# Two column blocks per bank in the output projections, new planner estimates, and queries rotated before their norm, in an fp32 two-layer encoder trunk

## The chip, the cores and the metric

The kernel is one program on one core of a Trainium2 chip. The metric is the device time of one execution in microseconds (us), taken as the median over runs.

## The reference, cut to what matters

Two layers over a sequence of 256 rows of 1024 features, all in float32. Each layer is: half a SwiGLU feed-forward (2816 wide), a mixer, cross-attention to a memory of 256 rows, half a feed-forward. The first mixer joins differential attention and stick-breaking attention; the second is latent attention (MLA):

```python
def mla_mixer(h, w_dq, q_lat_norm, w_uq, w_dkv, kv_lat_norm, w_ukv, qk_norm_q, qk_norm_k, w_o):
    c_q = rms_norm(h @ w_dq, q_lat_norm)
    q = to_heads(c_q @ w_uq, MLA_HEADS)
    dkv = h @ w_dkv
    c_kv = rms_norm(dkv[..., :MLA_KV_RANK], kv_lat_norm)
    kv = to_heads(c_kv @ w_ukv, MLA_HEADS)
    ...
    q = rms_norm(q, qk_norm_q)
    q = jnp.concatenate([q[..., :MLA_NOPE_DIM], rope(q[..., MLA_NOPE_DIM:])], axis=-1)
    o = chunk_causal_softmax_attention(q, k, v, MLA_QK_DIM ** -0.5)
    return from_heads(o) @ w_o

def diff_stickbreak_mixer(...):
    ...
    mixed = jnp.concatenate([from_heads(oa), from_heads(ob)], axis=-1)
    return mixed @ w_out

def memory_cross_attention(...):
    ...
    return from_heads(o) @ w_o
```

A rotation of a head's 32 rotary features and the division of the whole head by its own norm commute, since the norm is one number per row and head.

## The kernel before

All products are made from two fp32r halves of each operand: `mm3` (L285) issues three matmuls, high by high (L286), low by high (L287), high by low (L288). Weights arrive by DMA in float32; `issue` (L237) splits each into `wh` (a cast on ScalarE, L250) and `wl` (a subtraction on VectorE, the last 512 columns of a mixer's weight on GpSimd, L252). Three weights have room at once (`HL`), so a weight's split waits for the last use of the weight three before it.

The residual x is kept feature-major: 8 blocks of 128 features by 256 rows. The output projection of each mixer and of each cross-attention is `out_g` (L653). It goes over the 8 output blocks (`dt`) and over groups of source tiles, each with an event that says when the group is there (4 groups in a mixer, 2 in a cross-attention). Each `dt` accumulates in a PSUM bank of its own, taken from the 3 banks of kind "mm" (`BANKS`; the eight banks are 3 "mm", 2 "s" for scores, 2 "t" for transposes, 1 "o"). The first three blocks are open at once and take each group as it comes; the other five go one at a time. After the last group of a block, `finish_dt` (L506) adds the bank to x on VectorE (L510), makes the high half of the next phase's operand on ScalarE (L481) and the low half on VectorE (L482), and squares x for the next norm (L522, summed on GpSimd at L530). Then `drop` hands the bank back.

Only TensorE's order is written out by the kernel. Each piece of work is a generator that yields what it needs (events, a weight, a bank) and a latency; `run` (L437) keeps a clock of its own, to which every matmul adds an estimate (`spend`), and takes the ready piece of the highest priority. When an event counts as signalled is set by the tables EST_X0, EST_X1, EST_AB and EST_MLA, in us behind the instruction that signals it. The other engines' instructions are ordered by the scheduler of the framework, in the order in which it believes they become ready, and each engine runs its list in that order. GpSimd's powers (`rsqrt`, L465 and L467) make the inverse roots.

In the MLA mixer, `keys` (L1259) norms a half of the keys (sums of squares L1274 and L1275, power L467, products L1288 and L1290), `turn_k` (L1297) transposes them and copies them out of PSUM on ScalarE (L1305). `queries` (L1312) takes one product of 128 rows and 4 heads: scaled copy out of PSUM (L1319) and squares (L1322) on ScalarE, sums of squares (L1324), an addition (L1325) and a 4-wide power for the norm, and the rotation: a product with the cosines on VectorE (L1332), two with the sines on GpSimd (L1334), their sum on VectorE (L1337). Only the norm's inverse root is kept apart: it enters in the softmax as a factor. `attend` (L1401) transposes the queries of two heads at a time (L767), copies them out on VectorE (L1409), and makes the scores (L1422), the softmax (L745 to L760), the transposes of the weights, and the values (L1455). The weights of this mixer come in the order of MLA_ORDER. In the first mixer, `stick` (L1034) and `scores` (L1112) do the two kinds of attention, `turn_o` (L1182) turns the differential output, and `mem_k` (L809) makes the memory's keys, whose norm is the product L827 before their transposes.

## Time and profile before

| | |
|---|---|
| median of 3 runs | 1087.91 us (1087.11 to 1088.03) |
| the profiled execution | 1090.49 us |
| its span in the trace | 1088.8 us |
| mean granted TensorE clock | 0.995 |
| busy share | TensorE 98%, VectorE 71%, ScalarE 60%, GpSimd 18% |
| instructions | 23382 |

The span runs from the first to the last instruction of the profiled execution; the 1.7 us that its own time is longer lie around it. Stretches named in the prediction are us from the start of the span: 196 to 333 the first mixer, 333 to 384 the first cross-attention, 384 to 734 two feed-forwards, 734 to 865 the MLA mixer, 865 to 916 the second cross-attention.

### The profile page before, as it was taken

The page shows a single profiled execution, that of the slowest core. Times are in us where ns is not written, and L with a number is a line of the kernel's source. Part 1 is how long each engine was busy: PE and PEld are TensorE (multiplying, and loading weights), DVE is VectorE, ACT ScalarE, POOL GpSimd, SP SyncE. Part 2 cuts the span into 40 slices and gives each one's busy share as a digit, 9 for nine tenths or more (in the row PEclk, how much of TensorE's full clock was granted, in tenths as well). Part 3 has the DMA queues.
Part 4 walks back from the last instruction along what each step waited for, and adds up shares of the span by engine and source line. Part 5 has one row for each costly group of instructions (what it writes and reads, how often), then busy time and mean ns, then how long its engine had stood idle before and what let it go on. Part 6 is the DMA issues. An engine that isn't in the chain of part 4 may idle for free.

```text
span 1088.8 us, 23382 instructions
## 1 busy us (share of the span) xinstructions
PE 1065.9 (98%) x9040; PEld 1046.5 (96%) x9040; DVE 769.4 (71%) x1866; ACT 655.4 (60%) x1775; POOL 192.5 (18%) x210
## 2 busy tenths in 40 slices
PE   9999999999989999999999999999989999999998
PEld 8899999998889999999999999999878999999998
DVE  5978766567867877776677777654678768777753
ACT  6666555576756765555565655555867567555542
POOL 1100001356245200000100000014861422000000
PEclk9999999999999999999999999999989999999999
DMA  8765555635346365545556555555342444555561
GB/s 291 248 223 209 195 198 186 195 116 161 111 126 199 107 219 179 211 177 198 185 194 219 193 215 179 202 186 161 110 131 64 144 145 167 205 190 198 184 220 63
DMA packets 50800, 193.36 MB, mean 178 GB/s; under 512 B 5760, under 2 KB 7552, under 8 KB 35584
## 3 DMA queue, kind: packets, MB, share of 16 engines
q1 hardware_dynamic: 50688, 191.86, 51.3%
q8 instruction: 71, 1.16, 0.4%
q14 instruction: 41, 0.34, 0.1%
HBM read 190.79 MB, written 1.05 MB: 176 GB/s over the span
## 4 chain that ended last, share of the span: by engine, by line
PE 87%; DVE 5%; ACT 2%; POOL 2%; DMA 2%; issue 1%; SPq 0%; DVEq 0%; ACTq 0%; POOLq 0%
PE mm L286 28%; PE mm L288 27%; PE mm L287 27%; DVE wl L252 2%; DMA wr<-wflat 2%; ACT slotf L754 1%; PE t L767 1%; POOL sm L467 1%; PE s L1422 1%; PE t L475 1%; PE s L892 0%; PE o L1455 0%; DVE sm L745 0%; ACT wh L250 0%; POOL sl L467 0%
## 5 line engine op out<-in xcount | busy, mean ns | idle before, releaser
L250 ACT CAST wh<-wr 128x256 fp32r<-128x256 f32 (+1 forms) x1216 | 441.2, 434 | 294.9 <-PE mm L287 237.8
L252 DVE TENSOR_TENSOR wl<-wr,wh 128x256 fp32r<-128x256 f32 (+1 forms) x1171 | 479.5, 464 | 122.1 <-ACT wh L250 117.1
L286 PE MATMUL mm<-xh,wh 128*128 128x256 f32 x1584 | 439.9, 278 | 3.8 <-DVE slotf L705 2.6
L288 PE MATMUL mm<-xh,wl 128*128 128x256 f32 x1584 | 437.6, 276 | 0.1
L287 PE MATMUL mm<-xl,wh 128*128 128x256 f32 x1584 | 437.4, 276 | 0.0
L286 PEld LDWEIGHTS mm<-xh,wh 128*128 128x128 f32 x1584 | 298.3, 188 | 5.0 <-issue 2.8
L287 PEld LDWEIGHTS mm<-xl,wh 128*128 128x128 f32 x1584 | 298.4, 188 | 0.6
L288 PEld LDWEIGHTS mm<-xh,wl 128*128 128x128 f32 x1584 | 298.1, 188 | 0.7 <-DVE wl L273 0.4
L286 PE MATMUL mm<-slotr,wh 128*128 128x256 f32 x896 | 247.6, 276 | 0.3 <-ACT slotr L481 0.3
L287 PE MATMUL mm<-slotr,wh 128*128 128x256 f32 x896 | 246.6, 275 | 0.4 <-DVE slotr L482 0.4
L288 PE MATMUL mm<-slotr,wl 128*128 128x256 f32 x896 | 246.5, 275 | 0.0
L286 PEld LDWEIGHTS mm<-slotr,wh 128*128 128x128 f32 x896 | 168.2, 188 | 1.0 <-ACT slotr L481 0.6
L287 PEld LDWEIGHTS mm<-slotr,wh 128*128 128x128 f32 x896 | 168.2, 188 | 0.7 <-DVE slotr L482 0.6
L288 PEld LDWEIGHTS mm<-slotr,wl 128*128 128x128 f32 x896 | 168.2, 188 | 0.0
L530 POOL TENSOR_TENSOR acc<-acc,sq 128x256 f32<-128x256 f32 x49 | 38.7, 790 | 455.0 <-ACT sq L522 452.9
L252 POOL TENSOR_TENSOR wl<-wr,wh 128x512 fp32r<-128x512 f32 x45 | 67.4, 1497 | 110.3 <-ACT wh L250 92.2
L713 DVE TENSOR_TENSOR slotf<-mm,rb 128x512 f32<-128x512 f32 x44 | 30.4, 690 | 59.4 <-PE mm L288 59.4
L481 ACT ACTIVATE xh<-x,gains 128x256 fp32r<-128x256 f32 x64 | 32.1, 507 | 29.8 <-DVE x L510 25.8
L705 DVE TENSOR_TENSOR slotf<-mm,rb 128x512 f32<-128x512 f32 x44 | 30.3, 689 | 23.4 <-PE mm L288 23.2
L754 ACT ACTIVATE slotf<-s,sm,sl 128x256 f32<-128x256 f32 (+1 forms) x64 | 32.8, 522 | 23.3 <-DVE sm L748 17.8
L510 DVE SCALAR_TENSOR_TENSOR x<-mm,x 128x256 f32<-128x256 f32 x64 | 26.7, 418 | 23.5 <-PE mm L288 23.3
L482 DVE SCALAR_TENSOR_TENSOR xl<-x,gains,xh 128x256 fp32r<-128x256 f32 x64 | 37.5, 590 | 5.3 <-ACT xh L481 5.2
(196 smaller groups left out, 1152.7 us busy)
## 6 DMA issues: line engine op xcount, KB each, us to landing
wr<-wflat SPq DMA_DIRECT2D x118, 1024.0 KB, 4.9
wr<-wflat SPq DMA_DIRECT2D x180, 256.0 KB, 3.9
wr<-wflat SPq DMA_DIRECT2D x16, 768.0 KB, 4.2
slotf<-memT SPq DMA_DIRECT2D x8, 256.0 KB, 3.4
x<-xT SPq DMA_DIRECT2D x4, 256.0 KB, 4.9
wr<-wflat SPq DMA_DIRECT2D x2, 512.0 KB, 8.2
slotf<-xtok SPq DMA_DIRECT2D x4, 256.0 KB, 7.8
...
```

What stands on the lines that cost most here:

```text
L250: A.copy(hi[:, a:b], raw[:, a:b])
L252: e.tensor_tensor(out=lo[:, a:b], in0=raw[:, a:b], in1=hi[:, a:b].bitcast(F32), op=ALU.subtract)
L286: PE.matmul(out, a[0], b[0], start=first, stop=False, **kw)
L287: PE.matmul(out, a[0], b[1], start=False, stop=False, **kw)
L288: PE.matmul(out, a[1], b[0], start=False, stop=last, **kw)
L481: return (A.activation(hi, src, AF.Identity, scale=g), V.scalar_tensor_tensor(out=lo, in0=src, scalar=g, in1=hi.bitcast(F32), op0=ALU.mult ...
L482: V.scalar_tensor_tensor(out=lo, in0=src, scalar=g, in1=hi.bitcast(F32), op0=ALU.mult, op1=ALU.subtract))
L510: V.scalar_tensor_tensor(out=xd, in0=ps, scalar=factor, in1=xd, op0=ALU.mult, op1=ALU.add)
L530: G.tensor_tensor(out=st.acc, in0=st.acc, in1=sq, op=ALU.add)
L705: V.tensor_tensor(out=t.rearrange("p (a b) -> p a b", b=S), in0=pg.rearrange("p (a b) -> p a b", b=S), in1=rbb, op=ALU.mult)
L713: V.tensor_tensor(out=u.rearrange("p (a b) -> p a b", b=S), in0=pu.rearrange("p (a b) -> p a b", b=S), in1=rbb, op=ALU.mult)
L754: A.activation(p[:, i * w:(i + 1) * w], sps[:, i * w:(i + 1) * w], AF.Exp, bias=nb[:, i:i + 1], scale=r, accum_out=sums[:, i:i + 1])
```

## The change

`out_g` puts two neighbouring 256-column blocks into one 512-column bank. The start flag is set only by the first matmul of the even block, the bank is dropped after the odd block, and six blocks are open at once before the other two go one at a time. The estimates of the planner get new values, two latencies in `mem_k` and `turn_k` as well, the f32 slots of the MLA arena go from 29 to 30, and MLA_ORDER brings both first query weights ahead of the second key/value weight. In `queries` the rotation now comes first, in spare columns of z and sq, the sums of squares behind it, and one addition and one 8-wide power serve both row blocks of a query group (four 8-wide powers for eight 4-wide ones).

```diff
-SLOTS_MLA = (29, 11)
+SLOTS_MLA = (30, 11)
-EST_AB = {..., 'va': 1.47, ..., 'sp': 3.0, ..., 'srco': 1.25}
+EST_AB = {..., 'va': 2.8, ..., 'sp': 4.4, ..., 'srco': 2.2}
-MLA_ORDER = (('k', 0), ('kv', 0), ('kv', 1), ('q', 0), ('q', 1), ('k', 1), ('q', 2), ('q', 3), ('v', 0))
+MLA_ORDER = (('k', 0), ('kv', 0), ('q', 0), ('q', 1), ('kv', 1), ('k', 1), ('q', 2), ('v', 0), ('q', 3))
...
-        spend(3 * 0.109 * b[0].shape[-1] / 256)
+        spend(3 * 0.115 * b[0].shape[-1] / 256)
...
             w = ws[dt // per]
             j = dt % per
+            ps = pss[dt // 2]
             for i, k in enumerate(rows_):
-                mm3(pss[dt][:, 0:S], (w[0][:, k, j * P:(j + 1) * P], w[1][:, k, j * P:(j + 1) * P]),
-                    src[i], g == 0 and i == 0, g == len(groups) - 1 and i == len(rows_) - 1)
+                mm3(ps[:, dt % 2 * S:dt % 2 * S + S], (w[0][:, k, j * P:(j + 1) * P], w[1][:, k, j * P:(j + 1) * P]),
+                    src[i], g == i == dt % 2 == 0, g == len(groups) - 1 and i == len(rows_) - 1,
+                    skip_group_check=True)
...
-                ps = pss.pop(dt)
-                finish_dt(dt, gc, ps[:, 0:S])
-                drop(ps, 0.8)
-        nw = BANKS["mm"]
+                finish_dt(dt, gc, ps[:, dt % 2 * S:dt % 2 * S + S])
+                if dt % 2:
+                    drop(ps, 0.8)
+        nw = 2 * BANKS["mm"]
...
-                    yield dict(after=[ev], w=keyf(dt // per), mm=int(g == 0))
+                    yield dict(after=[ev], w=keyf(dt // per), mm=int(g == 0 and dt % 2 == 0))
...
-            yield dict(t=1, lat=7.0)
+            yield dict(t=1, lat=9.0)
...
-            v = sm()[:, 0:4]
-            V.tensor_reduce(out=v, in_=sq[:, 0:384]...)
-            V.tensor_scalar(out=v, in0=v, scalar1=96 * EPS, ...)
-            rsqrt(v, 4, rqs[n][:, t * 4:(t + 1) * 4])
...
-            m1 = tmp[:, 0:128].rearrange("p (a b) -> p a b", b=32)
-            m2 = tmp[:, 128:256].rearrange("p (a b) -> p a b", b=32)
+            m1 = z[:, 384:512].rearrange("p (a b) -> p a b", b=32)
+            m2 = sq[:, 384:512].rearrange("p (a b) -> p a b", b=32)
...
             V.tensor_tensor(out=qr, in0=m1, in1=m2, op=ALU.add)
+            V.tensor_reduce(out=qv[n][:, t * 4:(t + 1) * 4], in_=sq[:, 0:384]...)
+            if t:
+                v = qv[n][:, 0:8]
+                V.tensor_scalar(out=v, in0=v, scalar1=96 * EPS, ...)
+                rsqrt(v, 8, rqs[n])
```

EST_MLA changes in eleven places (k 6.43 to 9, q 7.82 to 8, qT 2.38 to 3, cs 3.11 to 2, sp 6.25 to 4.6, p1 3.36 to 4.4, p2 0.68 to 1.2, o 0.58 to 2.2, src 0.8 to 1.6, pk 2.4 to 1.6, kT 0.9 to 1.5), EST_X0 and EST_X1 in "o" (to 1.6) and "src" (8.83 to 2.0). Lines of the changed kernel behind `out_g` have numbers 4 or 5 higher: L1409 becomes L1414, L1290 becomes L1294; in `queries`, L1332 becomes L1331, L1334 becomes L1333, L1337 becomes L1336, and the sums of squares L1324 become L1337.

Three places of the order show what moved. The first is TensorE in the first mixer's output projection, where one output block ends (its last group) and the next one begins, before and then now; mm is the bank, slotr the source, wh and wl the weight's halves.

```order
L286 MATMUL mm_4082<-slotr_2682,wh_3889 128x256
L287 MATMUL mm_4082<-slotr_2682,wh_3889 128x256
L288 MATMUL mm_4082<-slotr_2682,wl_3890 128x256
L286 MATMUL mm_4089<-slotr_2682,wh_3889 128x256
L287 MATMUL mm_4089<-slotr_2682,wh_3889 128x256
L288 MATMUL mm_4089<-slotr_2682,wl_3890 128x256
```

```order
L286 MATMUL mm_4076<-slotr_2682,wh_3895 128x256
L287 MATMUL mm_4076<-slotr_2682,wh_3895 128x256
L288 MATMUL mm_4076<-slotr_2682,wl_3896 128x256
L286 MATMUL mm_4076<-slotr_2682,wh_3895 128x256 [waits DVE_49]
L287 MATMUL mm_4076<-slotr_2682,wh_3895 128x256
L288 MATMUL mm_4076<-slotr_2682,wl_3896 128x256
```

Before, the next block is in another bank (mm_4089 behind mm_4082). Now it is in the same one (mm_4076), and its first matmul waits for VectorE. The VectorE instruction that it waits for is the addition L510 of the block that has just ended.

The second is VectorE in the MLA mixer around the first copies of transposed queries, L1409 before and L1414 now; t is the transposes' bank.

```order
L1332 TENSOR_TENSOR slotf_9734<-slotf_9737,mqa 128x128 [waits Activation_49]
L252 TENSOR_TENSOR wl_10426<-wr_10424,wh_10425 128x512 [waits DMAHW3_49,PE_49,Activation_49]
L1324 TENSOR_REDUCE sm_10404<-slotf_9742 128x4 [waits Activation_49]
L1337 TENSOR_TENSOR slotf_9737<-slotf_9734 128x4x32 [waits DVE_49,Pool_49]
L1325 TENSOR_SCALAR sm_10404<-sm_10404 128x4 [waits DVE_49]
L252 TENSOR_TENSOR wl_10426<-wr_10424,wh_10425 128x512 [waits DMAHW4_49,Activation_49]
L1409 COPY slotf_9743<-t_10461 96x512 [waits PE_49]
L1409 COPY slotf_9740<-t_10467 96x512 [waits PE_49]
```

```order
L1331 TENSOR_TENSOR slotf_9741<-slotf_9741,mqa 128x128 [waits Activation_49]
L1336 TENSOR_TENSOR slotf_9741<-slotf_9741,slotf_9742 128x4x32 [waits DVE_49,Activation_49,Pool_49]
L1337 TENSOR_REDUCE sm_10268<-slotf_9742 128x4
L1331 TENSOR_TENSOR slotf_9743<-slotf_9743,mqa 128x128 [waits Activation_49]
L252 TENSOR_TENSOR wl_10301<-wr_10299,wh_10300 128x512 [waits DMAHW0_49,PE_49,Activation_49]
L1336 TENSOR_TENSOR slotf_9743<-slotf_9743,slotf_9744 128x4x32 [waits DVE_49,Activation_49,Pool_49]
L1337 TENSOR_REDUCE sm_10268<-slotf_9744 128x4
L252 TENSOR_TENSOR wl_10301<-wr_10299,wh_10300 128x512 [waits DMAHW1_49,Activation_49]
L1341 TENSOR_SCALAR sm_10268<-sm_10268 128x8 [waits DVE_49]
L1278 TENSOR_REDUCE sm_10340<-slotf_9721 128x8 [waits Activation_49]
L1414 COPY slotf_9722<-t_10355 96x512 [waits PE_49]
```

Before and now, the copy of the first query group's transposes (t_10461, now t_10355) stands behind the rotations of the second group; now the key's sum of squares L1278 stands ahead of it as well.

The third is GpSimd in the same stretch, from the weight half behind the first keys' products on.

```order
L252 TENSOR_TENSOR wl_10187<-wr_10185,wh_10186 128x512 [waits DMAHW3_49,PE_49,Activation_49]
L467 TENSOR_TENSOR sm_10223<-sm_10220,small 128x8 [waits DVE_49]
L1290 TENSOR_TENSOR slotf_9748<-slotf_9727,sm_10223 128x4x32 [waits Pool_49]
L1290 TENSOR_TENSOR slotf_9749<-slotf_9727,sm_10223 128x4x32
L467 TENSOR_TENSOR sm_10249<-sm_10246,small 128x8 [waits DVE_49]
L1290 TENSOR_TENSOR slotf_9729<-slotf_9727,sm_10249 128x4x32 [waits Pool_49]
L1290 TENSOR_TENSOR slotf_9730<-slotf_9727,sm_10249 128x4x32
L252 TENSOR_TENSOR wl_10269<-wr_10267,wh_10268 128x512 [waits DMAHW7_49,PE_49,Activation_49]
L1334 TENSOR_TENSOR slotf_9735<-slotf_9724,mqb 128x4x16 [waits Activation_49]
L1334 TENSOR_TENSOR slotf_9735<-slotf_9724,mqb 128x4x16
L467 TENSOR_TENSOR sl_10295<-sm_10298,small 128x4 [waits DVE_49]
```

```order
L1294 TENSOR_TENSOR slotf_9735<-slotf_9718,sm_10169 128x4x32
L252 TENSOR_TENSOR wl_10177<-wr_10175,wh_10176 128x512 [waits DMAHW3_49,PE_49,Activation_49]
L1333 TENSOR_TENSOR slotf_9737<-slotf_9736,mqb 128x4x16 [waits Activation_49]
L1333 TENSOR_TENSOR slotf_9737<-slotf_9736,mqb 128x4x16
L1333 TENSOR_TENSOR slotf_9740<-slotf_9739,mqb 128x4x16 [waits Activation_49]
L1333 TENSOR_TENSOR slotf_9740<-slotf_9739,mqb 128x4x16
L252 TENSOR_TENSOR wl_10242<-wr_10240,wh_10241 128x512 [waits DMAHW7_49,PE_49,Activation_49]
L467 TENSOR_TENSOR sl_10204<-sm_10203,small 128x8 [waits DVE_49]
L1333 TENSOR_TENSOR slotf_9742<-slotf_9741,mqb 128x4x16 [waits Activation_49]
```

Before, two more powers and four products for keys stand between the first weight half and the first rotation; now the rotations of the first query group follow it directly, and behind them another weight half, one 8-wide power and the second group.

## Rows read from the trace of the kernel before

**Rows 1.** The page, part 1: busy time and share of the span, instructions of TensorE.

```profile
PE 1065.9 (98%) x9040; PEld 1046.5 (96%) x9040; DVE 769.4 (71%) x1866; ACT 655.4 (60%) x1775; POOL 192.5 (18%) x210
```

**Rows 2.** Windows (stretch: length, PE, PEld, DVE, ACT, POOL busy, PEclk, DMA share, GB/s).

```profile
196.00:333.00 137.00, 130.31 (x1114) 125.41 (x1113) 97.02 (x180) 89.04 (x203) 63.66 (x59) 1.00 0.46 144
333.00:384.00 51.00, 50.43 (x409) 48.87 (x408) 39.56 (x97) 33.63 (x91) 17.43 (x17) 1.00 0.44 151
384.00:734.00 350.00, 350.00 (x3085) 349.89 (x3085) 249.06 (x631) 204.57 (x590) 12.67 (x15) 1.00 0.56 196
...
765.00:800.00 35.00, 30.10 (x186) 27.07 (x185) 22.11 (x48) 24.15 (x44) 29.97 (x32) 0.94 0.35 115
800.00:865.00 65.00, 62.98 (x488) 57.70 (x487) 53.84 (x136) 43.07 (x119) 20.13 (x23) 0.98 0.32 103
865.00:916.00 51.00, 50.43 (x410) 49.02 (x409) 38.97 (x97) 33.80 (x91) 17.60 (x18) 1.00 0.44 153
```

**Rows 3.** Windows around the two longest gaps of PE.

```profile
298.00:303.00 5.00, 2.77 (x25) 2.56 (x24) 4.10 (x6) 3.64 (x8) 4.20 (x4) 1.00 0.44 125
795.00:804.00 9.00, 8.01 (x33) 7.45 (x34) 7.43 (x17) 5.23 (x16) 4.67 (x4) 0.62 0.44 150
```

**Rows 4.** Waits of PE in 196:333 (us in total, times, longest).

```profile
PE t L767 <- DVE slotf L827: 2.2, 1, 2.2
PE s L323 <- ACT slotf L754: 1.9, 2, 1.0
PE o L1079 <- issue: 0.9, 1, 0.9
PE o L1079 <- ACT slotf L991: 0.9, 1, 0.9
```

**Rows 5.** Waits of PE in 734:916.

```profile
PE s L1422 <- DVE slotf L1409: 2.6, 1, 2.6
PE t L767 <- ACT slotf L1305: 1.4, 1, 1.4
...
PE o L911 <- DVE slotf L775: 0.6, 1, 0.6
```

**Rows 6.** Timeline of all engines, 317.2:319.9, the diff/stick mixer's output projection.

```profile
317.91 0.28 PE L288 MATMUL mm<-slotr,wl 128*128 128x256 f32 x1
...
318.02 0.28 PE L286 MATMUL mm<-slotr,wh 128*128 128x256 f32 x1
...
318.22 0.42 DVE L510 SCALAR_TENSOR_TENSOR x<-mm,x 128x256 f32<-128x256 f32 x1 [2.35 <-PE mm L288]
...
318.68 0.51 ACT L481 ACTIVATE xh<-x,gains 128x256 fp32r<-128x256 f32 x1 [3.68 <-DVE x L510]
```

**Rows 7.** Groups by line over the whole span (busy, mean ns; idle before).

```profile
L482 DVE SCALAR_TENSOR_TENSOR xl<-x,gains,xh 128x256 fp32r<-128x256 f32 x64 | 37.5, 590 | 5.3 <-ACT xh L481 5.2
```

**Rows 8.** Groups by line and shape, window 755:830 (busy, mean ns; idle before).

```profile
L252 DVE TENSOR_TENSOR wl<-wr,wh 128x512 fp32r<-128x512 f32 x23 | 18.9, 835 | 6.3 <-ACT wh L250 6.3
...
L252 POOL TENSOR_TENSOR wl<-wr,wh 128x512 fp32r<-128x512 f32 x9 | 12.5, 1391 | 4.0 <-ACT wh L250 4.0
...
L1334 POOL TENSOR_TENSOR slotf<-slotf,mqb 128x64 f32<-128x64 f32 x16 | 7.3, 476 | 12.8 <-ACT slotf L1319 12.8
L467 POOL TENSOR_TENSOR sm<-sm,small 128x8 f32<-128x8 f32 x4 | 6.9, 1730 | 1.9 <-DVE sm L584 0.9 <-DVE sm L1275 0.8
...
L1409 DVE COPY slotf<-t 96x512 f32<-96x512 f32 x8 | 5.3, 675 | 0.2 <-PE t L767 0.2
...
L1324 DVE TENSOR_REDUCE sm<-slotf 128x4 f32<-128x384 f32 x8 | 4.3, 541 | 0.0
...
L1274 DVE TENSOR_REDUCE sm<-slotf 128x8 f32<-128x512 f32 x4 | 2.7, 673 | 0.0
...
L1337 DVE TENSOR_TENSOR slotf<-slotf 128x128 f32<-128x128 f32 x8 | 2.2, 279 | 4.1 <-POOL slotf L1334 4.1
```

**Rows 9.** Timeline of POOL, 772.2:773.5.

```profile
772.28 1.18 POOL L1290 TENSOR_TENSOR slotf<-slotf,sm 128x128 f32<-128x128 f32 x2
```

**Rows 10.** Timeline of PE, 759.7:760.0, first product with the latent key/value weight.

```profile
759.73 0.39 PE L286 MATMUL mm<-wh,slotr 128*128 128x512 f32 x1
```

More of the change, by code (lines that the diff above doesn't have):

```diff
@@ L677, in out_g @@
                 for dt in win:
-                    yield dict(after=[ev], w=keyf(dt // per), mm=int(g == 0))
+                    yield dict(after=[ev], w=keyf(dt // per), mm=int(g == 0 and dt % 2 == 0))
                     if dt // per not in ws:
                         ws[dt // per] = weight(keyf(dt // per), per * P)
-                    if g == 0:
-                        pss[dt] = take("mm")
+                    if g == 0 and dt % 2 == 0:
+                        pss[dt // 2] = take("mm")
                     part(dt, g)
@@ L1306, in turn_k @@
                 kT[hf].append(d)
-                drop(pt, 0.9)
+                drop(pt, 1.5)
                 signal(ev["kT", hf, g], EST_MLA["kT"])
@@ L1315, in queries @@
             if t == 0:
-                qf[n], rqs[n] = [], sl()
+                qf[n], qv[n], rqs[n] = [], sm(), sl()
             z = al()
@@ L1322, in queries @@
             A.activation(sq[:, 0:384], z[:, 0:384], AF.Square)
-            v = sm()[:, 0:4]
-            V.tensor_reduce(out=v, in_=sq[:, 0:384].rearrange("p (a b) -> p a b", b=96), axis=AX.X, op=ALU.add)
-            V.tensor_scalar(out=v, in0=v, scalar1=96 * EPS, scalar2=None, op0=ALU.add)
-            rsqrt(v, 4, rqs[n][:, t * 4:(t + 1) * 4])
             qr = z[:, 0:384].rearrange("p (a b) -> p a b", b=96)[:, :, 64:96]
-            tmp = al()
-            m1 = tmp[:, 0:128].rearrange("p (a b) -> p a b", b=32)
-            m2 = tmp[:, 128:256].rearrange("p (a b) -> p a b", b=32)
+            m1 = z[:, 384:512].rearrange("p (a b) -> p a b", b=32)
+            m2 = sq[:, 384:512].rearrange("p (a b) -> p a b", b=32)
             ta, tb = tabs["mq"]
@@ L1337, in queries @@
             V.tensor_tensor(out=qr, in0=m1, in1=m2, op=ALU.add)
-            rel(sq, tmp)
+            V.tensor_reduce(out=qv[n][:, t * 4:(t + 1) * 4], in_=sq[:, 0:384].rearrange("p (a b) -> p a b", b=96),
+                            axis=AX.X, op=ALU.add)
+            if t:
+                v = qv[n][:, 0:8]
+                V.tensor_scalar(out=v, in0=v, scalar1=96 * EPS, scalar2=None, op0=ALU.add)
+                rsqrt(v, 8, rqs[n])
+            rel(sq)
             signal(ev["q", n, t], EST_MLA["q"])
```

10 lines of the change are left out of this document (5 added, 5 removed).

## The prediction

> **What bounds the kernel now.** I read the page first, then windows by stage, then TensorE's waits in the stages that are not full. TensorE is busy 98% of the span [rows 1], so only its idle time can be won, and the windows say where that is [rows 2]: the two feed-forwards between 384 and 734 have none (350.00 of 350), the first mixer has 6.7 us (137 less 130.31), each cross-attention 0.6 (51 less 50.43), the MLA mixer 4.9 and 2.0. To the MLA mixer a second loss belongs: TensorE ran at 0.62 of its clock from 795 to 804, between its levels of 2.4 and 1.2 GHz, which is 9 x 0.38 = 3.4 us [rows 3]. In all 6.7 + 1.2 + 6.9 + 3.4 = 18.2 us, 1.7% of the time, is the most that a better order can give.
>
> The waits name what is late. First mixer [rows 4]: 2.2 for the normed memory keys, 1.9 for two scores' banks, 1.8 for the stick-breaking values; 0.8 is in smaller waits. MLA mixer [rows 5]: 2.6 for a score behind the copy of its queries (L1409), 1.4 for a transposes' bank (L1305). In the cross-attention the wait is 0.6 at the values (L911).
>
> **Part 1, two blocks per bank.** The reader should look at the seam between an even block and its odd partner. Before, the last matmul of a block started at 317.91 and the first of the next block, in another bank, at 318.02 [rows 6]. Meanwhile L510 started at 318.22 and took 0.42, and the engine behind it started 0.04 after its end, at 318.68. Now the odd block's last group (or, for the two late blocks, its first) waits for that L510. TensorE can go on no earlier than 318.68 in place of 318.02: 0.66 per pair at least. The order shows such a wait at every pair: 4 pairs x 4 projections = 16, and TensorE has no other work between the two halves in any. The floor is 16 x 0.66 = 10.6 us.
>
> It costs more where VectorE isn't free. Lay out the first mixer's projection from the last matmul of block 0 at zero: L510 ends at 0.73, TensorE resumes at 0.77 and does block 1 (6 matmuls, 0.7) and block 2 (0.7), ended at 2.2. VectorE has by then L482 of block 0 (0.59 [rows 7], not before L481's 0.51: ended 1.9), L510 of block 1 (2.3), a weight piece (0.84 [rows 8]: 3.1), and only then L510 of block 2, ended 3.5. TensorE waits 1.3 instead of 0.66. By the same layout the third pair waits 1.0, and the fourth 1.5, as three weight pieces stand ahead of its L510: 0.7 + 1.3 + 1.0 + 1.5 = **4.5 us**. The MLA projection has the same order, one weight piece less at the end: **4.2**. The cross-attentions split their weights in smaller pieces: **3.2** each. Together 15.1, between 10.6 and, with one more weight piece of 0.84 ahead of half of the 16, 22.
>
> The Trainium skill (PSUM — Partial Sum Buffer, "PSUM bank collisions raise a hardware error") says that two engines may not touch one bank and quadrant at once, disjoint columns included, and tells to guard by bank, not by address. The instructions of the changed kernel are guarded so; a guard by address would take the 15.1 out of the sum. No run here shows a collision.
>
> What the six open blocks bring is small: the blocks' first groups no longer wait for a bank, so more matmuls are ready while the mixer's last source is made. In the cross-attentions the cover for the first source becomes thinner in layer 0 (6 matmuls) and better in layer 1: I take 1.5 of waits there for the two, where the two stretches had 1.2 idle [rows 2]. Cross-attentions: 0.3 + 6.4 = **+6.7 us**.
>
> **Part 2, the first mixer's order.** The longer latencies (9 for memory keys, 2.8 for "va", 4.4 for scores) put other matmuls ahead of the transposes and values that waited: 2.2 + 1.8 + 0.8 go, and one of the two waits for scores' banks (0.9) [rows 4]. New: a stick-breaking product has 12 matmuls less ahead of it and waits about 1.0 (0.3 to 2.5) for VectorE's halves, and a score's bank is behind a run of weight casts on ScalarE, 1.2 (0.5 to 2). One wait for scores stays, 1.0. The fourth weight chunk is released 24 matmuls (2.7 us) before its first use instead of 78; its third piece would come over 2 us late, but the seams just before hold TensorE back by as much, so I cost it at nothing. Idle after: 1.0 + 1.2 + 1.0 + 4.5 = 7.7 for 6.7: **+1.0**, between -4 and +3.
>
> **Part 3, queries and the MLA order.** Eight 4-wide powers become four 8-wide ones; as one of these takes 1.73 [rows 8], GpSimd saves little by it. What counts is its queue. Count from GpSimd's products for the first keys, ended 773.46 [rows 9], which the change leaves where they are. Then come, in the order shown, a weight half 1.39, four rotations 4 x 0.48, a weight half 1.39, a power 1.73, four rotations 1.90 [rows 8]: 782.2. VectorE adds the last rotation (0.28), reduces (0.54), splits a weight piece (0.84), adds the constant (0.16, an estimate: about half of L1337), reduces a key's squares (0.67) and then copies the first query group's transposes (0.68): 785.4.
>
> When does TensorE want that bank? The first product of the key/value weight starts at 759.73 [rows 10]. From there to the second transposes of queries the new order has 42 matmuls of 512 columns, 48 of 384 and 22 small ones; at 0.115 per 256 columns that is 9.7 + 8.3 + 2.5 = 20.5, so 780.2. It waits **5.2 us**, from 780.2 to 785.4: the planner's "q" and "qT" (8 and 3) don't know GpSimd's queue. Behind it the same again: the next copy stands behind a key's products that wait for GpSimd's next two powers (782.2 + 1.39 + 2 x 1.73 = 787.1, two products of about 0.54 and the copy: 788.8), wanted at 785.4 + 2.3 = 787.7: **1.1**. The third score then waits for a bank whose maximum stands behind two copies and three weight pieces on VectorE (1.35 + 2.5): **2.7**, between 1.3 and 3.5. After the 5.2 the clock falls to its lower level, as it did in the rows after the waits of 1.4 and 2.6; part of the 3.4 is hidden in the two waits that follow, I take **1.0**. What is late next: the values' sources and the last two sources of the projection have under 1 us of cover; I take **3.0** for the second half where the row has 2.0. With the banks 5.2 + 1.1 + 2.7 + 1.0 + 3.0 + 4.2 = 17.2 for 6.9 + 3.4 = 10.3: **+6.9**, between -3 and +13.
>
> Moved instructions on other queues: SP loads the query weights ahead of the second key/value weight, and the loads aren't late in any row that I rest on; the one extra f32 slot, the smaller change in `spend` and the two latencies in "src" act by the order only. The feed-forwards are not touched: nothing.
>
> **Sum.** +1.0 + 6.7 + 6.9 = +14.6 on the profiled execution's 1090.49: 1105.1. That execution is 2.6 us above the median of the runs, so 1087.91 + 14.6 = **1102.5 us**. Under 0.2% (2.2 us) a measurement can't tell from no change.
>
> **Rivals.**
> *The re-estimated order works* (slower still, by less). If GpSimd and VectorE take the queries before the weight pieces, so that the copy ends by 780.2, the waits of 5.2, 1.1, 2.7 and the clock's 1.0 are gone: 1102.5 - 10.0 = 1092.5. For it: the new latencies are longer where the rows show waits [rows 4, 5]. Against it: the queues in the order shown, each price from a row. Chance 0.17.
>
> *Faster.* One mechanism: the idle of the two mixers is all hidden and the seam costs its floor only. The place is the mixers, the price up to 18.2 won against 10.6 paid: 1087.9 - 18.2 + 10.6 = 1080.3. It decides at the point where more than the seams' cost is won; at 13 of the 18 it gives 1085.5. Against it: the waits counted above; the seam cannot be hidden, as TensorE takes its instructions in order. Chance 0.10.
>
> *The clock falls in the projections too.* There TensorE is busy 8.3 of some 12.8 us in the mixers. If it falls once in each, 2 x 3.4 more: 1109.3. For it: it fell after the gaps of 1.4 and 2.6 [rows 3, 5]. Against it: a stretch with a gap of 2.2 and 2.77 busy of 5.00 stayed at 1.00 [rows 3], and no seam is over 1.5. Chance 0.13.
>
> *The seam isn't there*, since VectorE's read is tracked by columns and the wait means an older instruction: 1102.5 - 15.1 = 1087.4, no change. Against it: the wait stands at each pair and at no other place of the block. Chance 0.04.
>
> **The numbers.** The forecast has 0.56, its own range 1096 to 1109. With the unknown prices (-5 and -10 in the mixers' own terms, +7 in seams and +6 in MLA, not all at once) and the second and fourth case, 1091 to 1113 holds 8 in 10. Faster by over 0.2%: 0.10; within 0.2%: 0.05, from the fourth case and the edge of the second; slower: 0.85.
>
> **What would show it.** Right: in the waits of the changed kernel PE mm L286 <- DVE x L510 with some 16 times and 10 to 20 us; PE t L767 <- DVE L1414 with one wait of about 5; the normed memory keys (L831) gone from the list. Windows: the cross-attentions' idle at 3 to 4 in place of 0.6. Wrong: an L510 wait of under 8 us in all, or no wait over 2 us before a transposition of queries; then the MLA term is off, and the sum with it.

## The result, and the profile after

| | before | after |
|---|---|---|
| median, us | 1087.51 (1086.38 to 1088.03, 4 runs) | 1117.39 (1116.01 to 1117.95, 4 runs) |
| the profiled execution | 1090.49 | 1116.01 |
| its span | 1088.8 | 1114.3 |
| mean granted clock | 0.995 | 0.992 |

The changed kernel takes 1.0266 times as long, with an interval of 1.0249 to 1.0283, which is 27 to 31 us more; the two medians are 29.9 us apart. The forecast was 14.6. The two traces differ by 25.5 us only: the profiled execution of before was 3.0 above its median, that of after 1.4 below its own. Where these 4.4 us lie can be read from the last L510 of the first feed-forward, in before and in after:

```profile
195.14 0.42 DVE L510 SCALAR_TENSOR_TENSOR x<-mm,x 128x256 f32<-128x256 f32 x1
```

```profile
190.70 0.42 DVE L510 SCALAR_TENSOR_TENSOR x<-mm,x 128x256 f32<-128x256 f32 x1 [0.16 <-PE mm L288]
```

Up to here TensorE's order is the same in both kernels, matmul by matmul, and yet the execution of before is 4.4 us behind. It had waited for VectorE near the program's start, and its clock fell behind that wait; in after the same wait is 0.3 and the clock is at 1.00 in the same window. The second fence is that window, with the columns of [rows 2]; the wait is the longest of before, though [rows 3] has two others as the longest:

```profile
30.02 0.35 PE L286 MATMUL mm<-xh,wh 128*128 128x256 f32 x1 [2.64 <-DVE slotf L705]
```

```profile
28.00:36.00 8.00, 5.98 (x38) 6.01 (x39) 7.65 (x22) 5.19 (x15) 1.19 (x5) 0.79 0.69 224
```

This is the spread of single executions and not the change: of the kernels below that leave all of this part as it is, the one with new estimates for the MLA attention alone passes the same L510 at 195.12, the one with the first mixer's new estimates at 190.84. From this point to the end, after takes 25.5 + 4.4 = 29.9 us longer than before, the distance of the medians. It is these 29.9 that have to be explained.

The page of after, part 1, answers to [rows 1]:

```profile
PE 1074.0 (96%) x9040; PEld 1051.1 (94%) x9040; DVE 776.5 (70%) x1862; ACT 656.6 (59%) x1775; POOL 191.6 (17%) x206
```

The windows of after answer to [rows 2, 3] (stretch: length, PE, PEld, DVE, ACT, POOL busy, PEclk, DMA share, GB/s). The stages are the first mixer, cross-attention, feed-forwards, the MLA mixer in two parts, cross-attention:

```profile
196.00:340.00 144.00, 135.34 (x1148) 129.97 (x1147) 101.41 (x186) 92.61 (x210) 64.75 (x62) 1.00 0.45 141
340.00:395.00 55.00, 51.22 (x398) 48.59 (x398) 39.64 (x99) 34.09 (x94) 12.79 (x12) 1.00 0.38 134
395.00:745.00 350.00, 350.00 (x3089) 349.85 (x3088) 248.34 (x628) 202.84 (x585) 16.82 (x19) 1.00 0.57 197
...
776.00:811.00 35.00, 26.38 (x141) 22.98 (x140) 25.93 (x56) 18.31 (x43) 19.31 (x22) 0.82 0.32 106
811.00:885.00 74.00, 63.97 (x482) 57.31 (x481) 52.01 (x117) 43.89 (x113) 21.38 (x22) 0.98 0.24 77
885.00:945.00 60.00, 56.83 (x445) 54.82 (x445) 43.07 (x102) 37.19 (x99) 19.36 (x19) 0.98 0.44 153
```

TensorE's idle time is length less busy. The feed-forwards have none, as before. The first mixer has 8.7 (before 6.7), the cross-attentions 3.8 and 3.2 (0.6 each), the MLA mixer 8.6 and 10.0 (4.9 and 2.0). The clock of 0.82 says that the MLA mixer lost more than idle time.

The waits of PE over the whole span of after (waiter <- what it waited for: us in total, times, longest), in place of [rows 4, 5]:

```profile
PE mm L286 <- DVE x L510: 15.7, 16, 2.3
PE s L323 <- ACT slotf L758: 3.5, 2, 2.8
PE t L771 <- ACT slotf L1309: 2.8, 1, 2.8
PE t L771 <- DVE slotf L1414: 2.8, 1, 2.8
...
PE t L475 <- POOL acc L530: 1.6, 2, 0.8
```

The first row is the seam of the prediction, with its 16 times: 15.7 us that no row of before has. The next three have one wait of 2.8 each in the MLA mixer. The last is new as well: at the end of each cross-attention the transposing matmul L475 of the next norm waits for GpSimd's sum of squares, which comes after the last seam.

The same view for the first mixer, 196 to 340, and for the first cross-attention, 340 to 395:

```profile
PE mm L286 <- DVE x L510: 5.5, 4, 2.3
PE s L1067 <- ACT slotr L486: 1.0, 1, 1.0
...
```

```profile
PE mm L286 <- DVE x L510: 2.4, 4, 0.8
PE t L475 <- POOL acc L530: 0.8, 1, 0.8
PE mm L287 <- DVE slotr L487: 0.6, 1, 0.6
```

The rest of the first mixer is 8.7 - 5.5 = 3.2, as forecast. The MLA mixer's seams are 5.5 too, the second cross-attention's 2.4.

Now the first mixer's four seams, one by one. The timeline of PE in after, 315.6 to 322.9 (start, us, engine, line, tiles; in brackets the idle before it and its releaser) shows three:

```profile
316.72 0.38 PE L286 MATMUL mm<-slotr,wh 128*128 128x256 f32 x1 [0.52 <-DVE x L510]
...
319.40 0.39 PE L286 MATMUL mm<-slotr,wh 128*128 128x256 f32 x1 [1.01 <-DVE x L510]
...
322.72 0.39 PE L286 MATMUL mm<-slotr,wh 128*128 128x256 f32 x1 [1.64 <-DVE x L510]
```

Such a wait is counted from the modelled end of the matmul before, not from the time at which the next one could start; from start to start each seam is 0.16 longer. The four are 0.68, 1.17, 1.80 and 2.50, together 6.15 where 4.5 was laid out. What VectorE did before the third, and GpSimd beside it (timelines of after):

```profile
319.26 0.48 DVE L482 SCALAR_TENSOR_TENSOR xl<-x,gains,xh 128x256 fp32r<-128x256 f32 x1
...
320.41 0.42 DVE L510 SCALAR_TENSOR_TENSOR x<-mm,x 128x256 f32<-128x256 f32 x1
320.75 1.58 DVE L482 SCALAR_TENSOR_TENSOR xl<-x,gains,xh 128x256 fp32r<-128x256 f32 x1
322.25 0.41 DVE L510 SCALAR_TENSOR_TENSOR x<-mm,x 128x256 f32<-128x256 f32 x1
```

```profile
320.78 1.27 POOL L252 TENSOR_TENSOR wl<-wr,wh 128x512 fp32r<-128x512 f32 x1 [15.36 <-ACT wh L250]
```

The low half L482 that starts at 320.75 takes 1.58 us; at 319.26 it takes 0.48. It ends 0.28 behind GpSimd's weight half (320.78 + 1.27 = 322.05), and the L510 for which TensorE waits starts then, at 322.25. Before the fourth seam it is two weight pieces on VectorE: 2.92 us from 325.46 where the usual is 1.36, beside GpSimd's next weight half (325.35 to 326.70) and the first of its sums L530 (326.66 to 327.83). L510, which reads one operand from PSUM, takes 0.41 to 0.43 throughout. This is what the Trainium skill (SBUF — State Buffer, "Who interferes with whom") states: a VectorE instruction with two inputs in SBUF contends with a GpSimd instruction that reads SBUF, one with at most one such input, outside the two-port modes, does not. The trace agrees on both halves of the rule. The same section of the Trainium skill calls this contention an exclusive lock. The trace agrees there too, as L482 ends only when GpSimd's instruction has ended.

The MLA mixer's three waits, in the timeline of PE:

```profile
785.29 1.94 PE L771 MATMUL t<-cst,slotf 128*96 128x128 f32 x8 [2.83 <-ACT slotf L1309]
...
791.90 1.94 PE L771 MATMUL t<-cst,slotf 128*96 128x128 f32 x8 [2.79 <-DVE slotf L1414]
...
805.68 0.47 PE L323 MATMUL s<-mk,mq 128*128 128x128 f32 x1 [2.81 <-ACT slotf L758]
```

The first, 2.83, was in no term of the sum. TensorE wants a transposes' bank and ScalarE has not copied the keys before it (L1309). The timeline of ScalarE and SP's load (SPq: from issue to landing):

```profile
782.17 0.62 ACT L250 CAST wh<-wr 128x512 fp32r<-128x512 f32 x1 [2.38 <-DMA wr<-wflat]
...
784.03 0.62 ACT L250 CAST wh<-wr 128x512 fp32r<-128x512 f32 x1 [0.31 <-DMA wr<-wflat]
784.55 1.25 ACT L1309 ACTIVATE slotf<-t,small 96x512 f32<-96x512 f32 x2
```

```profile
779.50 6.79 SPq L248 DMA_DIRECT2D wr<-wflat  x7
```

The keys' copy stands behind casts of weights, and these wait for a load that SP could issue only at 779.50, just after VectorE had read the buffer's old contents for the last time (until 779.41). The copy starts at 784.55, and TensorE 0.74 later. ScalarE's two waits for the load, 2.38 and 0.31, are together nearly as long as TensorE's 2.83. VectorE was held up there as at the seams: its last two pieces took 2.59 instead of 1.36 beside a weight half of GpSimd's.

```profile
776.82 2.59 DVE L252 TENSOR_TENSOR wl<-wr,wh 128x512 fp32r<-128x512 f32 x2
```

```profile
777.12 1.74 POOL L252 TENSOR_TENSOR wl<-wr,wh 128x512 fp32r<-128x512 f32 x1
```

The second wait is the predicted one, for the copy of transposed queries (L1414): 2.8 and not 5.2 + 1.1. Both of its ends came later than laid out, counted from the end of GpSimd's products for the first keys (777.15 here). TensorE wanted the bank 12.0 behind that point and not 6.7, mostly by the first wait and the fall of the clock behind it. The copy was done 14.7 behind it and not 11.9, as GpSimd didn't run through: its power waited 2.18 for VectorE's L1341.

```profile
783.94 2.21 POOL L467 TENSOR_TENSOR sl<-sm,small 128x8 f32<-128x8 f32 x1 [2.18 <-DVE sm L1341]
```

```profile
791.17 0.67 DVE L1414 COPY slotf<-t 96x512 f32<-96x512 f32 x1
```

The third is the score's bank: 2.81 for 2.7.

The clock, in windows at the four places of after, behind the program's start, where the granted clock went to its lower level (columns as above):

```profile
784.50:788.00 3.50, 2.71 (x11) 2.46 (x12) 1.41 (x4) 3.50 (x7) 3.50 (x6) 0.54 0.64 219
791.30:794.80 3.50, 2.90 (x11) 2.64 (x12) 1.47 (x4) 0.68 (x1) 3.42 (x4) 0.54 0.67 225
805.00:811.90 6.90, 6.22 (x25) 5.78 (x26) 4.23 (x15) 3.89 (x17) 0.00 (x0) 0.52 0.36 130
883.50:887.00 3.50, 3.50 (x20) 3.50 (x19) 2.72 (x3) 2.41 (x6) 3.34 (x4) 0.54 0.86 289
```

Each is near 0.5, that is 1.2 GHz. Length times what is missing to 1 gives 1.6 + 1.6 + 3.3 + 1.6 = 8.1 us lost; [rows 3] had 3.4. The first three fall right at the three waits of 2.8, the fourth at the last seam of the MLA projection.

### The profile page after: what moved, and what is told of

Read it like the earlier page. It is cut to its first block, busy times and chain, and to the rows that moved or that the text cites. A ratio compares the mean times of both kernels' runs of the same rounds, so it can differ in the third digit from the quotient of the medians.

```text
span 1114.3 us, 23355 instructions
## 1 busy us (share of the span) xinstructions
PE 1074.0 (96%) x9040; PEld 1051.1 (94%) x9040; DVE 776.5 (70%) x1862; ACT 656.6 (59%) x1775; POOL 191.6 (17%) x206
## 4 chain that ended last, share of the span: by engine, by line
PE 83%; DVE 8%; ACT 3%; POOL 2%; issue 2%; DMA 2%; DVEq 0%; ACTq 0%; POOLq 0%
PE mm L286 27%; PE mm L287 26%; PE mm L288 26%; DVE wl L252 3%; ACT slotf L758 1%; DMA wr<-wflat 1%; DVE x L510 1%; PE t L771 1%; POOL sm L467 1%; DVE xl L482 1%; ACT wh L250 1%; PE t L475 1%; PE s L896 1%; PE o L915 0%; POOL acc L530 0%
## 5 line engine op out<-in xcount | busy, mean ns | idle before, releaser
L252 DVE TENSOR_TENSOR wl<-wr,wh 128x256 fp32r<-128x256 f32 (+1 forms) x1171 | 484.9, 470 | 121.8 <-ACT wh L250 112.9
L286 PE MATMUL mm<-slotr,wh 128*128 128x256 f32 x896 | 251.1, 280 | 16.5 <-DVE x L510 15.7
L287 PE MATMUL mm<-slotr,wh 128*128 128x256 f32 x896 | 248.1, 277 | 1.8 <-DVE slotr L487 1.8
L530 POOL TENSOR_TENSOR acc<-acc,sq 128x256 f32<-128x256 f32 x49 | 45.1, 920 | 454.2 <-ACT sq L522 451.4
L252 POOL TENSOR_TENSOR wl<-wr,wh 128x512 fp32r<-128x512 f32 x45 | 64.9, 1443 | 145.0 <-ACT wh L250 132.7
L510 DVE SCALAR_TENSOR_TENSOR x<-mm,x 128x256 f32<-128x256 f32 x64 | 26.9, 420 | 31.3 <-PE mm L288 31.0
L482 DVE SCALAR_TENSOR_TENSOR xl<-x,gains,xh 128x256 fp32r<-128x256 f32 x64 | 37.5, 590 | 4.7 <-ACT xh L481 4.7
```

The costliest lines, as they stand in the source:

```text
L252: e.tensor_tensor(out=lo[:, a:b], in0=raw[:, a:b], in1=hi[:, a:b].bitcast(F32), op=ALU.subtract)
L286: PE.matmul(out, a[0], b[0], start=first, stop=False, **kw)
L287: PE.matmul(out, a[0], b[1], start=False, stop=False, **kw)
L482: V.scalar_tensor_tensor(out=lo, in0=src, scalar=g, in1=hi.bitcast(F32), op0=ALU.mult, op1=ALU.subtract))
L510: V.scalar_tensor_tensor(out=xd, in0=ps, scalar=factor, in1=xd, op0=ALU.mult, op1=ALU.add)
L530: G.tensor_tensor(out=st.acc, in0=st.acc, in1=sq, op=ALU.add)
```

## The experiments

The theory: the seam is worth its 18 us wherever the pairs are, and the new order of the MLA mixer costs about 10 by itself. The rival: the waits stand in for one another, so that a part alone costs little, or a part only appears late because of another. All medians are in us; each ratio is to the kernel before on the same chip.

**The pairs alone**, put into the kernel before, and **the change without them**:

```diff
 (before)
-            mm3(pss[dt][:, 0:S], ...
+            mm3(ps[:, dt % 2 * S:dt % 2 * S + S], ...
...
-        nw = BANKS["mm"]
+        nw = 2 * BANKS["mm"]
```

> The kernel before with the changed output projection alone. Seam theory: 16 waits of PE on DVE L510 of 15 us or more in sum, 1104 to 1109 us. Order theory: less than 1097 us, since the waits fall into time that TensorE had idle.

```diff
 (after)
-            mm3(ps[:, dt % 2 * S:dt % 2 * S + S], ...
+            mm3(pss[dt][:, 0:S], ...
...
-        nw = 2 * BANKS["mm"]
+        nw = BANKS["mm"]
```

> The changed kernel with the output projection of before (one bank per block, three blocks open); tables, order and query rotation stay changed. Seam theory (the odd block's wait for L510 costs 16 to 19 us in the trace, and 1.6 more at the sums of squares behind it): 1096 to 1100 us, and no wait of PE on DVE L510 left. Order theory (the new order of the mixers is the main cost, the seams only fill idle time that would be there anyway): above 1107 us.

Pairs alone: 1110.67, ratio 1.0215 (1.0198 to 1.0232), +23.2. Its waits of PE:

```profile
PE mm L286 <- DVE x L510: 15.7, 16, 2.3
...
PE t L475 <- POOL acc L530: 1.6, 2, 0.8
```

They are those of after, and the time is 1.7 over the range expected. Its span is 20.3 longer than before's, and it was 3.1 ahead at the last L510 of the first feed-forward: 23.4 from there on, as the medians say. From start to start the seams are 18.3, with L530 19.9; the clock fell once more than in before, right behind the last seam of the MLA projection (0.57 in 878 to 882), which is 1.7; the last 1.8 are not explained. Without the pairs: 1102.41, 1.0138 (1.0117 to 1.0159), and no wait on L510. So the pairs cost 15.0 on top of the other edits and 23.2 without them. The last L510 of each stage, against that of before, says where the parts don't add up (us longer than before; feed-forwards are counted to the cross-attention ahead of them, and within them the distance changes by 0.1 at most):

| | first mixer | cross-attention | MLA mixer | cross-attention | sum |
|---|---|---|---|---|---|
| the pairs alone | 5.2 | 5.7 | 5.9 | 6.6 | 23.4 |
| the change without them | -3.6 | 3.0 | 12.7 | 0.8 | 12.9 |
| the change | 1.9 | 6.2 | 16.2 | 5.6 | 29.9 |

In the first mixer they do add up; behind it the whole is 2.5, 2.4 and 1.8 less than its parts. The waits say where some 3 us of the difference are. In the first cross-attention and from the MLA mixer on, all waits of PE but L510's are 2.5 + 15.6 = 18.1 without the pairs and 1.4 + 13.5 = 14.9 with them: with six blocks open, matmuls are ready where TensorE otherwise waits for a source (L486, L487) or a value. Why the rest is there stays open.

**Both blocks finished after the odd one**, which takes the wait away by taking away the read:

```diff
 (after)
-                finish_dt(dt, gc, ps[:, dt % 2 * S:dt % 2 * S + S])
                 if dt % 2:
+                    for h in range(2):
+                        finish_dt(dt - 1 + h, gc, ps[:, h * S:h * S + S])
                     drop(ps, 0.8)
```

> The changed kernel, but an even block is added to x only after the last matmul of its odd partner, so that no matmul stands between the two reads. Seam theory: the L510 waits at the seam vanish, 1096 to 1101 us, as with banks of their own. If what costs is two blocks per bank as such (late squares, late release of the bank), it stays above 1105 us.

1110.79, 1.0216 (1.0186 to 1.0245). The L510 wait is gone, and yet only 6.6 of 18.3 came back. The time is the one expected of the rival, and one of its reasons, the late squares, is there; most of the rest is a reason that neither theory had. Waits of PE:

```profile
PE mm L288 <- DVE wl L252: 6.5, 2, 3.9
...
PE t L475 <- POOL acc L530: 2.8, 2, 1.4
```

Without the seams TensorE reaches the last weight chunk of the mixers before VectorE has split it, and the wait for GpSimd's squares grows, as now two blocks' squares come at the end. The mean clock falls to 0.987: it was at its lower level in six places, which by the reckoning above loses 13.7 us where after loses 8.1. The prediction had said of that chunk that the seams cover its lateness; here the cover is off, and the lateness is 4 us at the longest.

**No work on GpSimd in the output projections:**

```diff
 (after)
-POOL_OF = {}
+POOL_OF = {"ab_o": 0, "mla_o": 0, "xq0": 0, "xq1": 0}
```

> The changed kernel with the last weight piece of the mixers' output projections and of the cross-attentions' query weights split on VectorE, none on GpSimd. The third and fourth seam of the mixers cost 1.8 and 2.5 us where the sum had 1.0 and 1.5, and there L482 took 1.58 us while GpSimd made a weight half. If VectorE is held up by GpSimd's instruction: L482 at 0.5 there, the third seams at 0.6 to 0.8, the waits for L510 at 12 to 14 in place of 15.7, although VectorE has one weight piece more. If it is VectorE's own queue: 16 us or more of such waits.

Waits of PE, and VectorE's timeline at the same third seam:

```profile
PE mm L286 <- DVE x L510: 10.7, 16, 1.5
```

```profile
320.99 0.47 DVE L482 SCALAR_TENSOR_TENSOR xl<-x,gains,xh 128x256 fp32r<-128x256 f32 x1
```

L482 takes 0.47 where it took 1.58, the third seam 0.70 in place of 1.80, and the L510 waits are 10.7 in place of 15.7: from start to start 13.3, between the floor of 10.6 and the 15.1 that was laid out. In the MLA projection the clock was at its lower level around the first two seams (0.52 in 869.5 to 873), and seams are shorter there: in the run further below that splits two other MLA weights on VectorE, with GpSimd at work in the projection as in after and the clock low, the L510 waits of that projection are 2.8 in place of 5.5. So the clean comparison is the first mixer, at full clock in both, where the four seams are 4.2 in place of 6.1, the fourth 1.66. That GpSimd holds VectorE back at the seams is thereby shown. The median, 1113.93, 1.0229 (1.0200 to 1.0259), is 3.5 below that of after, but the two intervals overlap; TensorE waits 1.1 for low halves (L482) and 0.6 for a weight half (L252) instead, which it did not in after.

**Order in the MLA mixer.** First all tables (and the latencies, the weight order, the slot) in the kernel before; then the rotation alone:

```diff
 (before)
-EST_X0 = {..., 'o': 1.32, 'src': 8.83}
+EST_X0 = {..., 'o': 1.6, 'src': 2.0}
...
-MLA_ORDER = (('k', 0), ('kv', 0), ('kv', 1), ('q', 0), ...
+MLA_ORDER = (('k', 0), ('kv', 0), ('q', 0), ('q', 1), ...
```

> The kernel before with the new planner estimates, latencies, weight order and 30 slots alone (old projection, old queries). Order theory of the prediction (MLA worse by some 7 to 10 us, first mixer better by 3): 1092 to 1098 us. If the new estimates are right and only the rotation or the banks hurt: 1080 to 1087 us.

```diff
 (before)
+            V.tensor_reduce(out=qv[n][:, t * 4:(t + 1) * 4], in_=sq[:, 0:384]...)
+            if t:
...
+                rsqrt(v, 8, rqs[n])
```

> The kernel before with the changed query code alone (rotation first, one 8-wide power per group). TensorE's order is the same as before, so only the other engines' queues differ. If the rotation helps as meant (queries' copies L1409 earlier, four powers fewer): 1083 to 1087 us, the wait of 2.6 for that copy smaller. If the sums of squares behind the rotation and the 8-wide power hold up the keys' powers on GpSimd: 1088 to 1092 us, with longer waits for transposes of keys.

Tables: 1099.13, 1.0112 (1.0094 to 1.0131), a little over the range expected. Rotation: 1086.55, 0.9992 (0.9979 to 1.0005), no difference that can be told. With the rotation alone TensorE's order is that of before, the wait of 2.6 at L1409 [rows 5] is gone, and in the MLA mixer waits of 2.4 at L827 and 1.9 at L759 have come in its place. So the loss of the MLA mixer is in the tables and not in the rewritten queries. Three of their parts, each alone:

```diff
 (before)
-MLA_ORDER = (('k', 0), ('kv', 0), ('kv', 1), ('q', 0), ...
+MLA_ORDER = (('k', 0), ('kv', 0), ('q', 0), ('q', 1), ...
```

> The kernel before with the new weight order of the MLA mixer alone (and its 30 slots). If the order of weights brings part of the loss: 1091 us or more, with a wait for transposes of queries of over 2 us. If only the estimates do: 1086 to 1089 us.

```diff
 (before)
-EST_MLA = {..., 'pk': 2.4, ..., 'k': 6.43, 'kT': 0.9, ...}
+EST_MLA = {..., 'pk': 1.6, ..., 'k': 9.0, 'kT': 1.5, ...}
...
-                drop(pt, 0.9)
+                drop(pt, 1.5)
```

> The kernel before with the new MLA estimates alone (old weight order, old queries, own banks). The tables-only kernel lost 11.7 us although its first mixer gained about 4. If the estimates bring the loss: 1097 to 1103 us, with waits of over 2 us for transposes' and scores' banks. If the weight order brings it: 1085 to 1090 us here.

```diff
 (before)
-EST_MLA = {..., 'cs': 3.11, 'sp': 6.25, 'p1': 3.36, 'p2': 0.68, ..., 'o': 0.58, 'src': 0.8}
+EST_MLA = {..., 'cs': 2.0, 'sp': 4.6, 'p1': 4.4, 'p2': 1.2, ..., 'o': 2.2, 'src': 1.6}
```

> The kernel before with the new MLA estimates of the attention alone (cs, sp, p1, p2, o, src); those of keys and queries (pk, k, kT, q, qT) as before. k_mla_tables_only lost 10.6 us, with one wait of 4.3 for a bank of key transposes and 6.7 for banks of scores. If the key and query estimates start it: 1087 to 1091 us. If too short a time for scores' banks (sp 4.6 for 6.25) is enough by itself: 1094 to 1099 us.

| edit alone | median | ratio |
|---|---|---|
| weight order | 1100.73 | 1.0115 (1.0091 to 1.0138) |
| EST_MLA and the drop | 1098.75 | 1.0105 (1.0090 to 1.0121) |
| EST_MLA, attention's part | 1100.22 | 1.0105 (1.0083 to 1.0126) |
| all tables | 1099.13 | 1.0112 (1.0094 to 1.0131) |

Each part alone costs about what all together cost. By the last L510 of each stage all of it is in the MLA mixer for the single parts (13.2, 9.8 and 10.9; in every other stage 0.1 at most). All tables cost 13.0 there, win 3.7 in the first mixer and lose 3.0 and 0.8 in the cross-attentions. Waits of PE, with the weight order alone and then with EST_MLA alone:

```profile
PE t L767 <- ACT slotf L1305: 4.1, 2, 3.3
PE t L767 <- DVE slotf L1409: 3.4, 1, 3.4
```

```profile
PE s L323 <- ACT slotf L754: 6.7, 4, 3.8
PE t L767 <- ACT slotf L1305: 4.3, 1, 4.3
```

Whichever part is moved, TensorE asks for transposes or scores before ScalarE (L1305, the softmax's L754) or VectorE (L1409) has come to the copy; once it stands there, a second early request stands behind the first. That is a reading of the waits; no run takes it further apart. The old estimates put back into the change should then bring little:

```diff
 (after)
-EST_MLA = {..., 'pk': 1.6, ..., 'k': 9.0, 'kT': 1.5, 'q': 8.0, ...}
+EST_MLA = {..., 'pk': 2.4, ..., 'k': 6.43, 'kT': 0.9, 'q': 7.82, ...}
...
-                drop(pt, 1.5)
+                drop(pt, 0.9)
```

> The changed kernel with the MLA estimates of before (weight order, queries, pairs and the first mixer's estimates stay changed). If the MLA estimates bring the second part of the loss: 1104 to 1110 us, that is 7 to 13 under the changed kernel, and no wait of PE in 770 to 815 over 3 us. If the weight order brings it: 1114 us or more.

1113.48, 1.0224 (1.0205 to 1.0242): 3.9 less than after, and nearer to what the weight order as the cause would give. The wait for the keys' copy shrinks to 1.1, and those for the queries' copy grow to 4.8 in two (one of 4.4), near the 5.2 of the prediction, with 3.3 more at the scores behind it. By the last L510 of each stage the MLA mixer takes 11.0 longer than in before, where after takes 16.2; 1.6 is lost again ahead of it, as the clock falls behind the first mixer's fourth seam, which it did not in after:

```profile
331.00:334.50 3.50, 3.50 (x19) 3.50 (x19) 2.74 (x4) 2.50 (x6) 3.34 (x4) 0.54 0.90 291
```

Less the mixer's seams, 6.1 in both, some 10 us of loss become some 5. So the MLA estimates bring about half of it; with the weights in the new order the rest stays, in other places.

**The first MLA wait: the load or ScalarE's order?** GpSimd's part of two MLA weights goes to VectorE, which was meant to free the buffer earlier or later:

```diff
 (after)
-POOL_OF = {}
+POOL_OF = {"ukv": 0, "uq": 0}
```

> The changed kernel with the last pieces of the MLA mixer's key/value and query weights split on VectorE in place of GpSimd. The first long wait of that mixer (2.8, for the copy L1309) was not in the sum: ScalarE stood before a cast whose weight landed late, behind a raw buffer that GpSimd read until 778.9. If that late load makes the wait: the raw buffer is free 1 us or more earlier and the wait at L1309 is under 2 us. If ScalarE's order alone makes it: 2.5 us or more.

1114.38, 1.0242 (1.0212 to 1.0272), not distinguishable from after. Waits of PE:

```profile
PE t L771 <- ACT slotf L1309: 3.4, 1, 3.4
```

VectorE now reads the buffer until 779.84, 0.4 later; but this execution was 0.4 later already at the end of the feed-forwards ahead of the mixer, so the buffer came free when it did in after. The wait is 0.6 longer mainly because TensorE comes 0.5 earlier by the same count. So the edit didn't move the load, and what an earlier load would win is not shown; that ScalarE stands 2.7 us at these casts in after is what speaks for the load. A third buffer was not tried.

**The first mixer's estimates**, alone; with pairs whose two even blocks end before the odd ones; and with the rotation:

```diff
 (before)
-EST_AB = {..., 'va': 1.47, ..., 'sp': 3.0, ..., 'srco': 1.25}
+EST_AB = {..., 'va': 2.8, ..., 'sp': 4.4, ..., 'srco': 2.2}
...
-            yield dict(t=1, lat=7.0)
+            yield dict(t=1, lat=9.0)
```

> The kernel before with the new estimates of the first mixer and the longer latency of the memory keys alone. The prediction's term for that mixer without seams was 3.5 us less idle: 1083 to 1085.5 us, with the waits for memory keys and stick-breaking values gone. If new waits take their place: 1086 to 1090 us.

```diff
 (the kernel above)
+            o = dt % 2 * S if dt < 4 else 0
+            ps = pss[dt // 2 * 2 if dt < 4 else dt]
...
-        for win in [tuple(range(nw))] + [(dt,) for dt in range(nw, KT)]:
+        for win in [(0, 1, 2, 3)] + [(dt,) for dt in range(4, KT)]:
...
-                for dt in win:
+                for dt in (0, 2, 1, 3) if g == last and len(win) > 1 else win:
```

> f with two blocks per bank in a first window of four blocks, whose last groups go 0, 2, 1, 3, so that six matmuls in another bank stand between a block's end and the matmul that waits for its L510; blocks 4 to 7 keep banks of their own. If it is the wait at the seam that costs, and not two blocks per bank: within 1.5 us of f, and under 1 us of waits for L510. If sharing a bank costs by itself: 5 us or more above f.

```diff
 (the first of these kernels)
-            yield dict(t=1, lat=9.0)
+            yield dict(t=1, lat=7.0 if l else 9.0)
...
+            V.tensor_reduce(out=qv[n][:, t * 4:(t + 1) * 4], in_=sq[:, 0:384]...)
```

> The kernel before with the new estimates of the first mixer, the longer latency of memory keys in layer 0 alone, and the changed query code. f won 3.7 us of waits in the first mixer and gave them back by a lower clock there and by one new wait of 2.6 for keys in the MLA mixer, which layer 1's longer latency caused. With that wait gone: 1083 to 1086 us, faster than before. If the gain of the first mixer is lost whatever stands in the second: 1087 to 1090 us.

The estimates alone: 1089.72, 1.0013 (0.9999 to 1.0027), where a gain was expected. The first mixer's idle time does fall, from 6.7 to 4.1, but the clock falls there once (0.72 in 300 to 306), the same latency of 9 acts on the memory keys of the second layer too, and the MLA mixer has a new wait of 2.4 for the keys (L767 <- L1290) and one of 2.0 at L827. The latency in the first layer alone, with the rotation: 1086.94, 0.9989 (0.9978 to 1.0001), no difference that can be told, and 1 us short of what was hoped for. With the even blocks ended first: 1093.75, 1.0062 (1.0039 to 1.0086), 4.0 above the same kernel without pairs. No L510 wait is left, but the waits of PE show two new rows:

```profile
PE mm L288 <- DVE wl L252: 2.6, 1, 2.6
...
PE mm L287 <- DVE xl L482: 2.2, 2, 1.1
```

TensorE reaches the last weight chunk and the low halves too early, as it did with both blocks finished after the odd one, and the clock falls in four places behind the program's start, two more than with the same estimates alone. No version tried beats the kernel before by more than the measurement can tell.

## Why the prediction was half right

The direction and the main mechanism were right, the size was not: 29.9 us where 14.6 were forecast. The prediction's own terms against the traces, in us over before, from the last L510 of the first feed-forward on:

| term | forecast | measured |
|---|---|---|
| the 16 seams | +15.1 | +18.3 |
| L530 behind the last seam of a cross-attention | none | +1.6 |
| rest of the first mixer, for 6.7 | -3.5 | -3.5 (3.2) |
| rest of the cross-attentions, for 1.2 | +0.3 | -0.6 (0.6) |
| waits of the MLA mixer, for 6.9 | +5.1 | +6.2 (8.6 + 10.0 - 5.5 = 13.1) |
| clock, for 3.4 | -2.4 | +4.7 (8.1) |
| sum | +14.6 | +26.7 of 29.9 |

**The seam** was right in mechanism, in number and in place, and the pairs alone show it. The cross-attentions' 3.2 each measured 3.04. The step that failed is the layout of the mixers' third and fourth seams, "the third pair waits 1.0, and the fourth 1.5": they were 1.80 and 2.50. VectorE's order was laid out rightly, but with durations that are means; [rows 7] gave 0.59 for an L482 that takes 0.48 alone and 1.58 beside GpSimd. With GpSimd out of the projections the third is 0.70.

**The clock** is the largest miss, 7.1 us. The step that failed is "part of the 3.4 is hidden in the two waits that follow, I take 1.0": one fall was counted for waits of 5.2, 1.1 and 2.7. There were four, 8.1 us. [rows 3, 5] had shown a fall after a gap of 2.6, and the forecast itself had a second wait of 2.7; at the 3.4 of [rows 3] for each, 6.8 less what the waits hide was to be expected. Two more falls came with a wait and a seam that the forecast did not have at this length (the keys' 2.8, the fourth seam's 2.5). The rival "the clock falls in the projections too" came true in one of its two places: the fourth seam of the MLA projection, not that of the first mixer.

**The MLA waits** came out 1.1 off in sum and wrong in make-up. The predicted chain through GpSimd's and VectorE's queues to the copy L1414 was seen, at 2.8; with the old estimates put back, and less wait ahead of it, it was 4.8. By the prediction's own prices GpSimd's queue ends at 781.8 and not 782.2, so the term was 4.8 and the forecast 1102.1. What failed is "the loads aren't late in any row that I rest on", which held for the rows of before and not for the new order: ScalarE's casts of a weight wait 2.38 for one, and the keys' copy is behind these casts. ScalarE's queue was not walked in the MLA mixer.

**Left out:** the next norm's sum of squares behind the last seam, 0.8 in each cross-attention. **Right:** the first mixer's rest, to 0.1 us; the feed-forwards untouched; a late weight chunk covered by the seams, seen when the cover was taken off; and that "GpSimd saves little" by the new queries: alone they change nothing that can be told. "What the six open blocks bring is small" holds, but 3 us is not nothing.

Not explained are 3.2 of the 29.9 us, and why the parts (23.2 for the pairs, 15.0 for the rest) add up to more than 29.9 by more than those 3.

## What to carry to other kernels

Two accumulations in one bank save a bank only if nothing reads the first before the second has ended; where the two end one behind the other, each pair costs at least the read's time on TensorE (0.68 here), and more when the reading engine has other work ahead or is held by GpSimd. An estimate that makes TensorE ask earlier was worth nothing here; every engine's queue in between has to be walked to the instruction that answers, the casts and loads in it included. A wait that may bring the clock down is to be priced with its fall, each such wait anew. And two traces are to be compared from an instruction ahead of the first change on: here 4.4 us of difference lay before it.
